# A one-element memset on GpSimd that waits for TensorE's reads ahead of the cast of keys, in an attention kernel

## Chip, cores and metric

The kernel runs on one core of a Trainium2 chip. The metric is device time in microseconds of one execution, the median of several. Times inside an execution come from a hardware profile of one run and count from the start of its span. Engines are named TensorE (PE in the profile, with its weight loads as PEld), VectorE (DVE), ScalarE (ACT), GpSimd (POOL) and SyncE (SP).

## What is computed

Plain softmax attention over 64 heads of 512 positions by 64 numbers, in float32 at both ends:

```python
batch, heads, seq, dim = 8, 8, 512, 64
scores = np.einsum('bhqd,bhkd->bhqk', q, k) * scale      # scale = 1 / sqrt(dim)
scores = scores - scores.max(axis=-1, keepdims=True)
attn = np.exp(scores)
attn = attn / attn.sum(axis=-1, keepdims=True)
return np.einsum('bhqk,bhkd->bhqd', attn, v).astype(np.float32)
```

## The kernel before

Two heads form a pair; there are 32 pairs, counted by `g`. For each pair the kernel does this:

1. SyncE loads q, k and v of the pair, 256 KB each (`load`, line 462), into float32 tiles, seven of each kind.
2. GpSimd casts them to 16 bits (`cast`): q and k into one tile `qkp` for the pair (line 478; the pool of these tiles has five buffers), v into one of twelve tiles `vp` (line 468). Pair 0 is handled apart, by `first_pair`.
3. TensorE transposes q and k out of `qkp` into PSUM in eight steps (`transposes`, line 502), and VectorE copies the result to SBUF as `tqk` (`copy`, line 515).
4. TensorE multiplies blocks of keys with the queries into score tiles `st` of 128x1024 in PSUM (`scores`, line 542), of which there are three buffers.
5. ScalarE takes the exponential of most score tiles (line 546). For 16 of them VectorE builds the exponential instead: `raise_` reads the scores out of PSUM (line 566), then five passes over 16-bit tiles in SBUF finish it (`pass_`, lines 583, 592, 600, 602, 606).
6. TensorE multiplies the exponentials with `vp` (`values`, line 638). VectorE takes a reciprocal of the sums (line 612) and normalises into the tile `ring` (line 617), and a store carries each head out.

The order of all this is made ahead of time, by the class `Plan`. It walks through time in steps of 5 ns with a cost for each kind of work and writes a list of steps; these are then issued in that order, and every engine works through its own queue in order. The plan casts pair `g` only when the transposes of pair `g - QK16`, with `QK16 = 5`, are over, since the five `qkp` buffers are used in turn.

A cast is also placed against VectorE's work. The plan emits it ahead of a VectorE step that works out of PSUM, and `cast_behind` ties it to the VectorE instruction recorded last (`latest`), with a dependency whose reason reads "SBUF ports". So a cast of GpSimd normally waits for up to four things: its load, that VectorE instruction, TensorE's transposes which read the old contents of its `qkp` buffer, and GpSimd's own earlier writes to that buffer. The last two fall to the cast of keys, which is the first to write the buffer; the cast of queries writes the other half behind it. GpSimd's queue executes a wait as a separate semaphore instruction when an instruction has more than it carries itself.

Of the kernel before, what the change touches and what calls it, by code (L numbers as in the profile page):

```python
# [9 lines left out]
FP32 = mybir.dt.float32  # L10
# [371 lines left out]
def kernel(  # L382
# [7 lines left out]
    nc = tc.nc  # L390
    B, H, S, D = q.shape
    P = 128
# [18 lines left out]
    cpool = ctx.enter_context(tc.tile_pool(name="const", bufs=1))  # L411
# [15 lines left out]
    ident = cpool.tile([P, P], FP16, name="ident")  # L427
# [3 lines left out]
    qkp = {}  # L431
    tqk = {}
    tps = {}
# [30 lines left out]
    def cast(g, name):  # L464
        if g >= NP:
            return
        if name == "v":
            return nc.gpsimd.tensor_copy(  # L468
                out=vps[g % NV][:, :, :, 0:D], in_=raw[g]["v"][:, :, :, :]
            )  # L470
        if g not in qkp:
            qkp[g] = qpool.tile([P, 2, NI, P], FP16, tag="qkp", name=f"qkp_{g}")
        dst = qkp[g][:, "qk".index(name)].rearrange("p i (h d) -> p h i d", h=2)
        src = raw[g][name]
        if (g, name) == (1, "q"):
            nc.vector.tensor_copy(out=dst[:, :, 0:2], in_=src[:, :, 0:2])
            return nc.gpsimd.tensor_copy(out=dst[:, :, 2:4], in_=src[:, :, 2:4])
        return nc.gpsimd.tensor_copy(out=dst, in_=src[:, :, :, :])  # L478

    latest = []
    SYNC = mybir.DependencyInfo(mybir.DependencyClass.Sync, mybir.DependencyReason.DATA)

    def dve(ins):
# [1 line left out]
        return ins  # L487

    def cast_behind(g, name, behind):
        ins = cast(g, name)  # L490
        if behind and latest:
            tc.add_manual_dep(ins.ins, latest[0].ins.name, SYNC, reason="SBUF ports")

    def transposes(g, n, bank):
        if n == 0:
            tqk[g] = tpool.tile([P, 2, S], FP16, tag="tqk", name=f"tqk_{g}")
        if n == 0 or g == 1:

            tps[g] = ps_x.tile([P, 2, NI, P], FP16, tag=f"x{bank ^ n}", name=f"tp_{g}_{n}")
        n = 1 - n  # L500
        for i in range(NI):
            nc.tensor.transpose(tps[g][:, n, i, :], qkp[g][:, n, i, :], ident)  # L502
        if g == 1 and n == 1:
            copy(g, n)

    def copy(g, n=0):
        if g == 1:
            dve(
                nc.vector.tensor_copy(
                    out=tqk[g][:, n], in_=tps[g][:, n].rearrange("p i c -> p (i c)")  # L510
                )
            )
            return
        dve(
            nc.vector.tensor_copy(  # L515
                out=tqk[g][:, :, :], in_=tps.pop(g).rearrange("p n i c -> p n (i c)")
            )
        )
# [258 lines left out]
    with tc.manual_schedule():  # L777
        plan = Plan(groups, NP, 3)
        steps = plan.run()
        first_loads()  # L780
        for g, name in plan.first_loads:
            load(g, name)
        make_identity(nc, ident)
        for n in range(NV):
            nc.vector.memset(vps[n][:, :, :, D : D + 1], 1.0)
        first_pair()
        do = {
            "transposes": transposes,
            "scores": scores,
            "values": values,  # L790
            "load": load,
            "store": store,
            "cast": cast_behind,
            "raise": raise_,
            "copy": lambda g, b: copy(g),
            "pass": pass_,
            "last": last_values,
            "finish": finish,
            "rec": lambda u, n, b: reciprocal(u, n),
            "mul": lambda u, n, b: normalise(u, n),  # L800
        }
        for what, *args in steps:
            do[what](*args)
# [30 lines left out]
```

## Time and profile before

| | |
|---|---|
| median of 3 runs | 115.96 us (115.36 to 116.09) |
| the profiled execution | 115.99 us, of which the span of instructions is 114.2 us |
| TensorE busy | 104.4 us, 91% of the span |
| VectorE busy | 103.3 us, 90% |
| ScalarE busy | 106.5 us, 93% |
| GpSimd busy | 56.8 us, 50% |
| granted TensorE clock, mean | 0.998 |
| casts of keys, line 478 | 31, 616 ns each |
| casts of queries, line 478 | 30, 616 ns each |
| casts of values, line 468 | 32, 619 ns each |

A row of the timeline gives the start and the duration in us, the engine, the line in the kernel, the operation, the tile written and the tile read, and in brackets the idle time of the engine before it with the instruction that ended it. A row of groups gives, behind the count, the busy time in us and the mean of one in ns, and then the idle time before the group's instructions. A row of one line's instructions gives the minimum, median and maximum in ns. A row of windows gives the stretch, its length, and the busy time of PE, PEld, DVE, ACT and POOL, each with its count, then clock, DMA share and rate. Recorded spans of one engine can overlap, since an instruction starts before the one ahead has ended.

### The profile page before, as it was taken

Reading aid. Unit: us, or ns where it says so; the run is one execution under the profiler, and the core shown is the slowest. Engines: PE = TensorE matmul, PEld = TensorE weight load, DVE = VectorE, ACT = ScalarE, POOL = GpSimd, SP = SyncE. Lnnn points to the kernel's source line nnn. Section 1 sums busy time; section 2 is a strip of 40 time slices with the busy share of each in tenths; the row PEclk is TensorE's granted clock in tenths of the full one; section 3 lists DMA queues with packets and bytes.
Section 4 is the critical chain, followed back from the end, with each engine's and each line's share of the span. In section 5 each row is a group of like instructions: output and inputs, shape, how many; then the busy total and the mean of one; then the engine's idle time right before and its main releaser. Section 6 shows DMA issues by size and latency. Waiting matters only on the chain.

```text
span 114.2 us, 4337 instructions
## 1 busy us (share of the span) xinstructions
PE 104.4 (91%) x1687; PEld 67.9 (59%) x1687; DVE 103.3 (90%) x226; ACT 106.5 (93%) x118; POOL 56.8 (50%) x101
## 2 busy tenths in 40 slices
PE   7966999999999889999999999999999999999950
PEld 2623566566856457666658557567675676577640
DVE  1557899999999999999999999999999999999660
ACT  4698999999999999999999999999999999999940
POOL 2156844785445744784473675655828374400000
PEclk9999999999999999999999999999999999999999
DMA  2899999999999999789899999999995993755243
GB/s 94 277 359 379 384 386 375 384 380 378 384 354 350 354 375 354 259 268 302 216 374 361 305 277 329 326 350 349 366 322 165 301 291 121 260 182 187 98 149 130
DMA packets 35381, 33.84 MB, mean 296 GB/s; under 512 B 2592, under 2 KB 35360, under 8 KB 35360
## 3 DMA queue, kind: packets, MB, share of 16 engines
q1 hardware_dynamic: 34928, 33.17, 87.3%
q10 hardware_dynamic: 432, 0.39, 1.0%
q8 instruction: 13, 0.21, 0.8%
q14 instruction: 8, 0.07, 0.2%
HBM read 25.17 MB, written 8.39 MB: 294 GB/s over the span
## 4 chain that ended last, share of the span: by engine, by line
DVE 50%; PE 20%; DMA 11%; ACT 9%; issue 4%; POOL 1%; SPq 1%; ACTq 0%
PE o L638 10%; DVE pd L566 10%; DVE tqk L515 10%; DVE ring L617 9%; ACT pt L546 9%; PE st L542 8%; DVE m L600 5%; DMA q<-in_q_dram 5%; DVE pd L606 4%; DMA out_dram<-ring 4%; DVE pe L592 3%; DMA v<-in_v_dram 3%; DVE rc L612 2%; DVE m L602 2%; DVE m L583 2%
## 5 line engine op out<-in xcount | busy, mean ns | idle before, releaser
L546 ACT ACTIVATE pt<-st 128x1024 f16<-128x1024 f32 (+1 forms) x110 | 101.3, 1054 | 0.7 <-PE st L542 0.3
L638 PEld LDWEIGHTS <-pt 128*128 128x128 f16 x880 | 38.7, 98 | 13.0 <-issue 10.6
L638 PE MATMUL o<-vp,pt 128*128 128x65 f16 x880 | 45.5, 194 | 0.7 <-DVE ring L617 0.2
L542 PE MATMUL st<-tqk 64*128 64x512 f16 (+1 forms) x250 | 42.5, 381 | 2.2 <-ACT pt L546 0.7
L478 POOL CAST qkp<-k 128x512 f16<-128x512 f32 x31 | 19.1, 616 | 16.5 <-DVE pe L592 4.2
L468 POOL CAST vp<-v 128x512 f16<-128x512 f32 x32 | 19.4, 619 | 14.3 <-DVE m L602 4.3
L478 POOL CAST qkp<-q 128x512 f16<-128x512 f32 x30 | 18.5, 616 | 9.0 <-DVE pe L592 2.4
L638 PE MATMUL o<-vp,pe 128*128 128x65 f16 x128 | 22.2, 195 | 0.2
L617 DVE TENSOR_TENSOR ring<-o,rc 128x448 f32<-128x448 f32 (+2 forms) x37 | 22.1, 599 | 0.1
L638 PE MATMUL o<-vp,pd 128*128 128x65 f16 x128 | 22.0, 193 | 0.1
L502 PEld LDWEIGHTS <-qkp 128*128 128x128 f16 x248 | 14.2, 97 | 10.9 <-issue 5.2
L502 PE MATMUL tp<-ident,qkp 128*128 128x128 f16 x248 | 19.6, 220 | 1.3 <-DVE tqk L515 0.6
L566 DVE TENSOR_SCALAR pd<-st 128x1024 uint16<-128x1024 f32 x16 | 19.4, 1213 | 1.0 <-PE st L542 1.0
L515 DVE COPY tqk<-tp 128x1024 f16<-128x1024 f16 x30 | 20.2, 676 | 0.0
L542 PEld LDWEIGHTS <-tqk 64*128 64x128 f16 x250 | 10.6, 93 | 11.1 <-issue 3.0
L638 PEld LDWEIGHTS <-pe 128*128 128x128 f16 x128 | 12.5, 98 | 2.9 <-issue 2.0
L638 PEld LDWEIGHTS <-pd 128*128 128x128 f16 x128 | 12.6, 98 | 0.4 <-DVE pd L606 0.2
L600 DVE TENSOR_TENSOR m<-m 128x1024 f16<-128x1024 f16 x16 | 12.6, 787 | 0.0
L606 DVE TENSOR_TENSOR pd<-pd,m 128x1024 f16<-128x1024 f16 x16 | 11.8, 739 | 0.0
L612 DVE RECIPROCAL rc<-o 128x7 f32<-128x7 f32 (+2 forms) x37 | 7.1, 192 | 1.3 <-PE o L638 1.3
L592 DVE TENSOR_SCALAR pe<-pd 128x1024 uint16<-128x1024 uint16 x16 | 7.1, 446 | 0.0
L583 DVE TENSOR_SCALAR m<-pd 128x1024 uint16<-128x1024 uint16 x16 | 6.9, 434 | 0.0
(49 smaller groups left out, 31.0 us busy)
## 6 DMA issues: line engine op xcount, KB each, us to landing
v<-in_v_dram SPq DMA_DIRECT2D x32, 256.0 KB, 5.5
k<-in_k_dram SPq DMA_DIRECT2D x31, 256.0 KB, 5.4
q<-in_q_dram SPq DMA_DIRECT2D x31, 256.0 KB, 5.3
out_dram<-ring SPq DMA_DIRECT2D x62, 128.0 KB, 2.9
k<-in_k_dram ACTq DMA_DIRECT2D x2, 128.0 KB, 2.9
q<-in_q_dram SPq DMA_DIRECT2D x2, 128.0 KB, 2.7
out_dram<-ring ACTq DMA_DIRECT2D x1, 128.0 KB, 1.7
out_dram<-obl SPq DMA_DIRECT2D x1, 128.0 KB, 1.7
```

The source lines that it names most:

```text
L468: return nc.gpsimd.tensor_copy(out=vps[g % NV][:, :, :, 0:D], in_=raw[g]["v"][:, :, :, :])
L478: return nc.gpsimd.tensor_copy(out=dst, in_=src[:, :, :, :])
L502: nc.tensor.transpose(tps[g][:, n, i, :], qkp[g][:, n, i, :], ident)
L515: nc.vector.tensor_copy(out=tqk[g][:, :, :], in_=tps.pop(g).rearrange("p n i c -> p n (i c)"))
L542: nc.tensor.matmul(st[:, x, cols], kc, qc[:, cols], start=True, stop=True)
L546: nc.scalar.activation(out=pt[:, :, cols], in_=st[:, :, cols], func=EXP, scale=scale, bias=SHIFT)
L566: nc.vector.tensor_scalar(out=r["pd"][:, :, :], in0=r["st"][:, :, :], scalar1=BITS, scalar2=BIAS, op0=AluOp.mult, op1=AluOp.add,)
L592: ins = nc.vector.tensor_scalar(out=r["pe"][:, :, :], in0=u[:, :, :], scalar1=0x7C00, scalar2=None, op0=AluOp.bitwise_and,)
L600: ins = nc.vector.tensor_tensor(out=m16, in0=m16, in1=m16, op=AluOp.mult)
L606: ins = nc.vector.tensor_tensor(out=u16, in0=u16, in1=m16, op=AluOp.mult)
L617: nc.vector.tensor_tensor(out=ring[:, u % NU : u % NU + n, :], in0=o[:, x : x + n, 0:D], in1=rcs.pop(u)[:, 0:n].broadcast_to([P, n, D]), o ...
L638: nc.tensor.matmul(os[u // 7][:, u % 7, :], part[:, y * P : (y + 1) * P], vps[g % NV][:, h, c, :], start=(n == 0), stop=(n == len(parts) - 1),
```

## The change

Ahead of the cast of keys of pair `g`, GpSimd now sets one element of a new tile `mark` to zero. A dependency makes this memset wait for the last transpose of pair `g - 5`, the pair that used the same `qkp` buffer before. `transposes` keeps that instruction in `reads`. As pair 0 has no such transposes, the first memset stands ahead of the cast of keys of pair 6, and there are 26 in all. Once the memset has waited, the cast behind it in GpSimd's queue needs no wait for TensorE.

```diff
     latest = []
+    reads = {}
+    mark = cpool.tile([P, 1], FP32, name="mark")
...
     def cast_behind(g, name, behind):
+
+
+        if name == "k" and g - Plan.QK16 in reads:
+            small = nc.gpsimd.memset(mark[0:1, :], 0.0)
+            tc.add_manual_dep(small.ins, reads[g - Plan.QK16].ins.name, SYNC, reason="tile")
         ins = cast(g, name)
         if behind and latest:
             tc.add_manual_dep(ins.ins, latest[0].ins.name, SYNC, reason="SBUF ports")
...
         for i in range(NI):
-            nc.tensor.transpose(tps[g][:, n, i, :], qkp[g][:, n, i, :], ident)
+            reads[g] = nc.tensor.transpose(tps[g][:, n, i, :], qkp[g][:, n, i, :], ident)
```

## Prediction

> **What bounds the kernel now.** I read the page's busy shares first, then the stretches by window, the chain that ended last, and only then the rows of single instructions around the casts.
>
> ```profile
> PE 104.4 (91%) x1687; PEld 67.9 (59%) x1687; DVE 103.3 (90%) x226; ACT 106.5 (93%) x118; POOL 56.8 (50%) x101
> DVE 50%; PE 20%; DMA 11%; ACT 9%; issue 4%; POOL 1%; SPq 1%; ACTq 0%
> ...
> 12.00:107.00 95.00, 92.00 (x1551) 60.88 (x1549) 94.70 (x191) 94.69 (x104) 51.78 (x88) 1.00 0.93 309
> 107.00:114.20 7.20, 3.10 (x75) 2.56 (x73) 2.69 (x8) 2.71 (x4) 0.00 (x0) 0.97 0.45 149
> ```
>
> The third number of a window row's busy times is VectorE, the fourth ScalarE. From 12 to 107 us VectorE is busy 94.70 of 95.00 us and ScalarE 94.69. VectorE has no gap to give, and its queue is in order; half of the chain is its own work. So whatever makes one VectorE instruction shorter moves all behind it, as far as ScalarE follows. The last 7.2 us are a tail that the change does not touch.
>
> ScalarE is as full, but not by work alone:
>
> ```profile
> 7.79 1.03 ACT L546 ACTIVATE pt<-st 128x1024 f16<-128x1024 f32 x1
> 9.17 8.36 ACT L546 ACTIVATE pt<-st 128x1024 f16<-128x1024 f32 x9 [0.34 <-PE st L542]
> ...
> 16.42 1.10 ACT L546 ACTIVATE pt<-st 128x1024 f16<-128x1024 f32 x1
> ...
> 17.33 1.11 ACT L546 ACTIVATE pt<-st 128x1024 f16<-128x1024 f32 x1
> ...
> 108.66 0.60 ACT L546 ACTIVATE pt<-st 128x512 f16<-128x512 f32 x1
> ...
> L546 ACT ACTIVATE pt<-st 128x1024 f16<-128x1024 f32 (+1 forms) x110 | 101.3, 1054 | 0.7 <-PE st L542 0.3
> ```
>
> When its scores are ready, one exponential follows another by 0.91 us (17.33 - 16.42), their recorded spans overlapping. The exponential at 16.42 is the tenth of 110 (one, then nine), the one at 108.66 the 109th. Between them lie 99 steps, or 90.1 us at 0.91, but 92.24 us pass. So about 2.1 us is the most that ScalarE can give back, in waits which the overlapping spans hide. That caps any gain here.
>
> **Where VectorE loses time.** Its passes over 16-bit tiles have a shortest and a usual length (minimum, median, maximum in ns):
>
> ```profile
> L583 DVE TENSOR_SCALAR m<-pd x16: 369/414/589, 11.1 to 103.3; 128x1024 uint16<-128x1024 uint16 x16
> L592 DVE TENSOR_SCALAR pe<-pd x16: 369/412/615, 13.7 to 104.2; 128x1024 uint16<-128x1024 uint16 x16
> L600 DVE TENSOR_TENSOR m<-m x16: 633/777/1033, 14.4 to 104.5; 128x1024 f16<-128x1024 f16 x16
> L602 DVE TENSOR_SCALAR m<-m x16: 369/422/501, 16.0 to 105.3; 128x1024 f16<-128x1024 f16 x16
> L606 DVE TENSOR_TENSOR pd<-pd,m x16: 640/706/921, 16.6 to 106.1; 128x1024 f16<-128x1024 f16 x16
> ```
>
> The long ones stand beside a cast of GpSimd. One place shows it:
>
> ```profile
> 16.64 0.68 DVE L606 TENSOR_TENSOR pd<-pd,m 128x1024 f16<-128x1024 f16 x1
> 17.24 0.68 DVE L515 COPY tqk<-tp 128x1024 f16<-128x1024 f16 x1
> 17.84 0.59 DVE L592 TENSOR_SCALAR pe<-pd 128x1024 uint16<-128x1024 uint16 x1
> 18.35 0.19 DVE L612 RECIPROCAL rc<-o 128x7 f32<-128x7 f32 x1
> 18.47 0.63 DVE L600 TENSOR_TENSOR m<-m 128x1024 f16<-128x1024 f16 x1
> ...
> 17.54 0.62 POOL L478 CAST qkp<-k 128x512 f16<-128x512 f32 x1 [1.43 <-DVE pd L606]
> 19.16 0.62 POOL L478 CAST qkp<-q 128x512 f16<-128x512 f32 x1 [1.01 <-DVE m L600]
> ...
> L478 POOLq EVENT_SEMAPHORE  x3: 17/17/43, 17.4 to 17.5; - x3
> ```
>
> A cast is released by the end of a chosen VectorE instruction, so that it runs beside a copy out of PSUM. The cast of keys was released at 17.32 (16.64 + 0.68) and began at 17.54, 0.22 us later; it then ran to 18.16, past the copy's end at 17.92, and the pass at 17.84 took 0.59 instead of 0.37. The cast of queries was released at 19.10 and began at 19.16, 0.06 us later. The difference is 0.16 us, and the last row names it: GpSimd's queue handles separate semaphore waits ahead of the cast of keys, one after the other, and starts that only when VectorE has finished.
>
> **The change part by part.** The built order of the changed kernel differs on GpSimd alone: 26 memsets, one ahead of each cast of keys from pair 6 on. Each takes over the wait for TensorE, and with it, from the second on, the wait for GpSimd's own earlier writes. The casts keep a DMA wait and mostly a VectorE wait, the form that casts of queries have; the first keeps one wait more. The order on TensorE, VectorE, ScalarE and the load queue is the same.
>
> *Gain.* In the trace, 15 of the 26 casts of keys start 0.22 us after the VectorE instruction that releases them; the first is at 17.54, the last at 92.58:
>
> ```profile
> 92.28 0.68 DVE L515 COPY tqk<-tp 128x1024 f16<-128x1024 f16 x1
> 92.88 1.21 DVE L566 TENSOR_SCALAR pd<-st 128x1024 uint16<-128x1024 f32 x1
> ...
> 91.89 0.62 POOL L478 CAST qkp<-q 128x512 f16<-128x512 f32 x1 [1.01 <-DVE pe L592]
> 92.58 0.62 POOL L478 CAST qkp<-k 128x512 f16<-128x512 f32 x1
> ...
> L478 POOL CAST qkp<-k 128x512 f16<-128x512 f32 x26 | 16.0, 616 | 13.8 <-DVE pe L592 4.2 <-PE st L542 2.7 <-DVE pd L606 2.2
> ```
>
> Ten of the fifteen have GpSimd idle before them for longer than 0.2 us, as at 17.54, and a delayed pass behind them, at once or after casts that follow without a gap: 10 x 0.16 = 1.6 us less delay on VectorE. The first keeps a separate wait for VectorE and saves about 0.1. Four come 0.02 to 0.07 us after the cast before (92.58 is one: 91.89 + 0.62 = 92.51), so GpSimd itself is free only then; they save 0.04 to 0.09 each, 0.3 together. Three more with fewer waits start 0.12 after their release and save 0.1 together. Sum 2.1 us.
>
> *Price.* The trace has no memset of one element. The nearest rows:
>
> ```profile
> 0.24 0.10 POOL L818 MEMSET const-float32-0.0<- 128x1 f32 x1 [0.24 <-issue]
> 0.27 0.10 POOL L818 MEMSET const-float32-1.0<- 128x1 f32 x1
> ...
> 0.73 0.20 POOL masks.py:197 MEMSET ident<- 128x128 f16 x1 [0.29 <-POOLq L818]
> ...
> 23.09 0.62 POOL L478 CAST qkp<-k 128x512 f16<-128x512 f32 x1
> 23.66 0.62 POOL L478 CAST qkp<-q 128x512 f16<-128x512 f32 x1
> ```
>
> One element per partition takes 0.10 us and delays the next memset by 0.03; a whole 128x128 tile takes 0.20. I take 0.04 of queue time, near the low end, since one element is nearest to those rows, with 0.03 and 0.20 as ends. In the idle places the memset runs right behind the cast before, over a microsecond ahead of the release, and costs GpSimd nothing; without that idle time it would cost its queue time. Behind it in GpSimd's queue stands the cast of keys, then those of queries and values, and the loads that reuse their tiles; none of them waits longer for TensorE than before, since the cast itself held that wait. Eight memsets stand between casts that follow each other closely (23.09 is such a cast of keys), where 0.04 shifts a pass by 0.02 to 0.04: 0.25. At about five places a 16-bit pass of VectorE is waiting for the cast ahead to end when the memset follows; between nothing and 0.10 each, I take 0.05: 0.25. Below nothing the price cannot be, as the memset replaces no work.
>
> The Trainium skill bears on these five. "SBUF — State Buffer", section "Who interferes with whom", says that a GpSimd instruction and a VectorE pass in a two-port mode exclude each other, for the whole instruction, whichever starts first. By it a memset that got in ahead would hold up the pass for all of its 0.10: 0.5 instead of 0.25, and the net on VectorE would be 1.35 us and the time 115.0. The same section lets VectorE instructions with two inputs in SBUF collide only with GpSimd instructions that read SBUF, which a memset does not.
>
> Net on VectorE: 2.1 - 0.25 - 0.25 = 1.6 us. How much of that reaches the end? At least VectorE's share of the chain, 50%; at most all, as 1.6 is under the 2.1 that ScalarE can give. I take three quarters, 1.2 us, for ScalarE's waits are spread over the whole span and follow VectorE's lateness. The profiled execution took 115.99 us (span 114.2 and 1.8 around it), so 115.99 - 1.2 = 114.8. The median of the runs shown is 115.96 (115.36 to 116.09), so the same sum holds for it: 1.0% faster. About 1% is also what a measurement of this kernel can tell from no change.
>
> **The rivals.**
> 1. *VectorE gains, the end hardly moves.* For it: TensorE is busy 92.00 of 95.00 us from 12 to 107, and half of the chain is not VectorE's. Against it: VectorE never waits there. A quarter of 1.6 arrives: 115.6.
> 2. *All of it arrives.* The memset is hidden everywhere and earlier casts also release transposes earlier; ScalarE gives back 1.9 of its 2.1: 114.1.
> 3. *Slower: the memset blocks.* It costs as much as the memset at 0.73, 0.20 us, and each of the 26 gets between VectorE's passes or pushes a cast out of its place: 26 x 0.20 = 5.2, less 2.1, is 3.1 lost, of which three quarters, 2.3, arrive: 118.3. It decides from 2.1 / 26 = 0.08 us a memset on. For it: GpSimd's casts do hold up VectorE (0.59 for 0.37). Against it: the rows of one element, and that most memsets fall in idle time.
> 4. *The change does not do what it says*, the cast still starts 0.22 late because something other than its separate waits delays it: 116.0.
>
> **How the numbers follow.** Forecast 0.45, rival 1 0.20, rival 2 0.18, rival 3 0.14, rival 4 0.03. The forecast's own range (a half to all of 1.6) is 114.4 to 115.2; 1% faster is 114.8, and I put 0.30 of its 0.45 on that side, as casts of queries and transposes behind an earlier cast of keys also gain. With rival 2 that is 0.48 for faster. Slower by over 1% is rival 3 but for its cheap end, 0.12. The rest is 0.40. The range goes from 113.9, just below rival 2 and the cap of 2.1, to 116.7, where each memset costs VectorE about 0.12 (26 x 0.12 - 2.1 = 1.0, three quarters of it 0.75); it leaves most of rival 3 out.
>
> **What would show it.** Casts of keys behind idle time start 0.06 us after their release; memsets take about 0.1 us and lie right behind the cast before; the five kinds of pass lose less (the medians above fall, the pass near 17.8 us to about 0.49, as the cast beside it saves 0.1); VectorE stays without gaps and ScalarE's last exponential comes 1.2 us earlier. Wrong would be: 0.22 still there (rival 4), the passes shorter but ScalarE's last exponential where it was (rival 1), or passes longer beside memsets (rival 3).

## The result, and the profile after

The changed kernel takes 115.03 us in the median of 20 executions, the kernel before 115.86 us in the median of 20. Over the executions that compare, the ratio is 0.993, with a 95% interval of 0.9912 to 0.9948: 0.7% faster, clear of the noise, and under the 1% that was forecast. The time lies inside the range of the prediction, but its larger chance, 0.48, stood on more than 1%; the measured gain falls to the 0.40 in the middle. In a later series the ratio was 0.9922 (0.9898 to 0.9946). One execution of the change, at 117.95 us and a granted clock of 0.967, is left out of the ratios.

Two executions of the changed kernel are profiled. The first (114.50 us, span 112.7) began its first casts some 0.4 us earlier than the profile before did, for its first loads came sooner. The second (114.66 us, span 112.9) started like the profile before, so the comparison is made with that one. The five kinds of pass and the memset there, as rows of one line's instructions (minimum, median, maximum in ns):

```profile
L590 DVE TENSOR_SCALAR m<-pd x16: 369/415/514, 11.1 to 102.0; 128x1024 uint16<-128x1024 uint16 x16
L599 DVE TENSOR_SCALAR pe<-pd x16: 368/375/586, 13.7 to 102.8; 128x1024 uint16<-128x1024 uint16 x16
L607 DVE TENSOR_TENSOR m<-m x16: 633/698/1033, 14.5 to 103.2; 128x1024 f16<-128x1024 f16 x16
L609 DVE TENSOR_SCALAR m<-m x16: 367/424/500, 16.0 to 103.9; 128x1024 f16<-128x1024 f16 x16
L613 DVE TENSOR_TENSOR pd<-pd,m x16: 635/692/771, 16.7 to 104.8; 128x1024 f16<-128x1024 f16 x16
...
L495 POOL MEMSET mark<- x26: 88/88/373, 16.1 to 91.1; 1x1 f32 x26
```

Lines 590, 599, 607, 609 and 613 are what 583, 592, 600, 602 and 606 were before. The shortest passes are as short as they were. Three of the five medians have come down (412 to 375, 777 to 698 and 706 to 692 ns), two have not moved, and the longest `m<-m` of 1033 ns stands ahead of the first memset. The place near 17.8 us, from the timeline:

```profile
16.70 0.68 DVE L613 TENSOR_TENSOR pd<-pd,m 128x1024 f16<-128x1024 f16 x1
17.30 0.68 DVE L522 COPY tqk<-tp 128x1024 f16<-128x1024 f16 x1
17.90 0.49 DVE L599 TENSOR_SCALAR pe<-pd 128x1024 uint16<-128x1024 uint16 x1
...
16.11 0.37 POOL L495 MEMSET mark<- 1x1 f32 x1
17.50 0.61 POOL L478 CAST qkp<-k 128x512 f16<-128x512 f32 x1 [1.02 <-issue]
```

The cast of keys is released at 17.38 (16.70 + 0.68) and starts at 17.50: 0.12 us later instead of 0.22, as this first cast keeps one separate wait. The pass behind it takes 0.49 instead of 0.59. The memset lies far ahead, in GpSimd's idle time. The next place shows the full step, first before, then after:

```profile
30.03 0.37 DVE L592 TENSOR_SCALAR pe<-pd 128x1024 uint16<-128x1024 uint16 x1
30.86 0.92 DVE L600 TENSOR_TENSOR m<-m 128x1024 f16<-128x1024 f16 x1
...
30.62 0.62 POOL L478 CAST qkp<-k 128x512 f16<-128x512 f32 x1 [1.50 <-DVE pe L592]
```

```profile
29.89 0.37 DVE L599 TENSOR_SCALAR pe<-pd 128x1024 uint16<-128x1024 uint16 x1
30.71 0.77 DVE L607 TENSOR_TENSOR m<-m 128x1024 f16<-128x1024 f16 x1
...
28.91 0.09 POOL L495 MEMSET mark<- 1x1 f32 x1
30.32 0.61 POOL L478 CAST qkp<-k 128x512 f16<-128x512 f32 x1 [1.32 <-DMA q<-in_q_dram]
```

Before, 0.22 us from the release (30.40) to the start; after, 0.06 (30.26 to 30.32). The pass behind it falls from 0.92 to 0.77 us. Before, two separate semaphore instructions ran behind the release, at 30.44 and 30.50. After, the cast still has one, for its load, but it ran at 28.40, ahead of the release, and costs nothing. (The bracket of the last row is the profile's guess; both loads of this pair had landed by 26 us.)

### The profile page after: what moved, and what is told of

It reads as the page before. It is cut to its first block, busy times and chain, and to the rows that moved or that the text cites. A ratio compares the mean times of both kernels' runs of the same rounds, so it can differ in the third digit from the quotient of the medians.

```text
span 112.7 us, 4366 instructions
## 1 busy us (share of the span) xinstructions
PE 103.6 (92%) x1687; PEld 67.7 (60%) x1687; DVE 102.2 (91%) x226; ACT 105.7 (94%) x118; POOL 58.7 (52%) x127
## 4 chain that ended last, share of the span: by engine, by line
PE 47%; DVE 38%; ACT 7%; issue 3%; DMA 1%; DVEq 0%; ACTq 0%
PE o L645 20%; PE st L549 17%; DVE pd L573 8%; DVE tqk L522 7%; ACT pt L553 7%; PE tp L509 7%; DVE ring L624 6%; DVE m L607 4%; PE st_0a L692 3%; DVE pd L613 3%; DVE pe L599 2%; DVE m L590 2%; DVE m L609 2%; DVE rc L619 2%; DMA out_dram<-ring 1%
## 5 line engine op out<-in xcount | busy, mean ns | idle before, releaser
L607 DVE TENSOR_TENSOR m<-m 128x1024 f16<-128x1024 f16 x16 | 11.6, 728 | 0.0
L613 DVE TENSOR_TENSOR pd<-pd,m 128x1024 f16<-128x1024 f16 x16 | 11.3, 707 | 0.0
```

The costliest lines, as they stand in the source:

```text
L607: ins = nc.vector.tensor_tensor(out=m16, in0=m16, in1=m16, op=AluOp.mult)
L613: ins = nc.vector.tensor_tensor(out=u16, in0=u16, in1=m16, op=AluOp.mult)
```

## The experiments

Each was timed over five rounds beside the kernel before on the same chip. The ratios are to that kernel, with 95% intervals.

**The wait on the cast ahead, without a memset.**

```diff
     latest = []
+    reads = {}
+    ahead = []
...
     def cast_behind(g, name, behind):
+        if name == "k" and g - Plan.QK16 in reads:
+            tc.add_manual_dep(ahead[0].ins, reads[g - Plan.QK16].ins.name, SYNC, reason="tile")
         ins = cast(g, name)
+        ahead[:] = [ins]
...
```

> No memset; the wait for TensorE's reads is put on the cast that stands just ahead of the cast of keys in GpSimd's queue. The cast of keys then has three waits instead of four, one separate semaphore instruction instead of two. Theory (the late start of the casts of keys is what VectorE pays): they start 0.12 us after their release instead of 0.22, up to 15 x 0.10 = 1.5 us less delay on VectorE, some of it lost where the cast ahead now starts 0.12 after its own release; about half arrives as with the changed kernel: 0.3 to 0.6 us faster than before, some 115.4. Rival (the memset itself, by breaking up GpSimd's queue, is what helps): no change, 115.9.

Measured: 115.33 us, ratio 0.9966 (0.9937 to 0.9995), so 0.4 us faster, as the theory had it. At the same place as above, from the timeline of this kernel:

```profile
30.66 0.37 DVE L597 TENSOR_SCALAR pe<-pd 128x1024 uint16<-128x1024 uint16 x1
31.49 0.82 DVE L605 TENSOR_TENSOR m<-m 128x1024 f16<-128x1024 f16 x1
...
31.16 0.62 POOL L478 CAST qkp<-k 128x512 f16<-128x512 f32 x1 [1.40 <-DVE pe L597]
```

The start is 0.13 us after the release (31.03), and the pass takes 0.82. With 0.22, 0.13 and 0.06 us of lateness the pass takes 0.92, 0.82 and 0.77: the lateness of the cast is passed on nearly in full. No memset is needed for a gain.

**The memset alone.** The dependency line of the change is left out.

> The 26 memsets stand where the change puts them but wait for nothing of TensorE; the casts of keys keep all their waits. Theory: the casts still start 0.22 us late, the passes stay as long as before, and the memsets cost 0 to 0.5 us on VectorE, so 115.9 to 116.3. Rival (the memset itself helps): about 115.0 like the changed kernel.

Measured: 115.10 us, ratio 0.9943 (0.9918 to 0.9968). The rival's number came out, but not for the rival's reason, and the expectation was wrong on what the edit does. All memsets write the same element, so each still waits for GpSimd's own writes up to the memset before it. That covers the wait for the older write of the buffer, and the casts of keys drop it. They start 0.12 us after their release, and the pass at the place above takes 0.82, as in the run before. The next run takes that apart.

**The memset apart from every wait.** As the run before, but each memset has an element of its own:

```diff
+    mark = cpool.tile([P, 32], FP32, name="mark")
...
+        if name == "k" and g - Plan.QK16 in reads:
+            nc.gpsimd.memset(mark[0:1, g : g + 1], 0.0)
```

> The 26 memsets wait for nothing and each sets an element of its own, so they carry no wait of GpSimd's own either, and the casts of keys keep all four waits and both separate semaphore instructions. This parts the memset from the waits, which the memset-only run did not: there the wait for GpSimd's own writes still moved to the memset, and the casts started 0.12 us after release. Theory: casts start 0.22 us late again, and what is left is the price of the memsets, 0 to 0.4 us slower than before: 115.8 to 116.2. Rival (a memset in the queue helps by itself): 115.1, as with the memset alone.

Measured: 116.13 us, ratio 1.0037 (1.0017 to 1.0057). The casts start 0.22 us late again and nothing is gained; the rival falls. At the same place the release is at 30.23 and the pass takes 0.92 again:

```profile
29.86 0.37 DVE L598 TENSOR_SCALAR pe<-pd 128x1024 uint16<-128x1024 uint16 x1
30.69 0.92 DVE L606 TENSOR_TENSOR m<-m 128x1024 f16<-128x1024 f16 x1
...
30.45 0.62 POOL L478 CAST qkp<-k 128x512 f16<-128x512 f32 x1 [1.48 <-DVE pe L598]
```

The kernel is even 0.4 us slower. Two more runs split that between the two kinds of place, with the condition in the edit above changed to lists of pairs.

> The memset alone cost 0.4 us in the run with all 26 apart from the waits. Here only the eight of them that stand between casts which follow each other closely; all casts of keys keep their four waits. Theory: the price lies here, 8 x 0.03 to 0.04 us of shift on VectorE and three quarters of it at the end: 0.2 us slower than before. Rival (the price lies where the memset meets a waiting pass, behind idle time): no change.

Measured, with the eight between close casts: 116.06 us, ratio 1.0028 (1.0007 to 1.0049).

> The other 18 memsets alone, those ahead of casts of keys that start after idle time or a release of VectorE; all casts of keys keep their four waits. Theory: 0 to 0.1 us slower than before. Rival (they get between VectorE's passes, 0.05 us and more at some five places, or push casts out of place): 0.3 to 0.4 us slower.

Measured, with the other 18: 116.05 us, ratio 1.0021 (0.9996 to 1.0046). The timings do not tell the two apart. In the profile of the first one the eight memsets, from 23.6 us on, delay VectorE by nothing to speak of: ahead of them it is already 0.48 us behind the profile before (a normalising instruction at 24.00 instead of 23.52), and at its last pass 0.49 (106.62 instead of 106.13). The profile of the second one shows a different culprit:

```profile
20.09 1.21 DVE L572 TENSOR_SCALAR pd<-st 128x1024 uint16<-128x1024 f32 x1
21.22 0.67 DVE L521 COPY tqk<-tp 128x1024 f16<-128x1024 f16 x1
21.82 0.19 DVE L618 RECIPROCAL rc<-o 128x7 f32<-128x7 f32 x1
21.93 1.06 DVE L612 TENSOR_TENSOR pd<-pd,m 128x1024 f16<-128x1024 f16 x1
...
21.34 0.09 POOL L495 MEMSET mark<- 1x1 f32 x1
21.84 0.61 POOL L478 CAST qkp<-k 128x512 f16<-128x512 f32 x1 [0.41 <-DMA k<-in_k_dram]
```

This is the cast of keys of pair 7. The VectorE instruction that releases it ended at 21.30, the memset was over at 21.43, and the cast waited on for its load, which landed at 21.69 (19.94 in the profile before). It then met a pass, which took 1.06 us instead of 0.65. Behind this place no VectorE instruction of this profile differs in length by more than 0.02 us from the profile before. So in these two traces the memsets cost nothing to speak of, and in the second a late load did. What makes the medians of the three versions with memsets apart from the waits 0.2 to 0.4 us slower stays open.

**Only where a cast is late.** The change, but with memsets only ahead of 18 of the casts of keys:

```diff
-        if name == "k" and g - Plan.QK16 in reads:
+        if name == "k" and g in (6, 7, 9, 10, 12, 13, 14, 16, 17, 18, 20, 21, 23, 24, 26, 28, 30, 31):
```

> As the change, but only ahead of the 18 casts of keys that start after idle time or a release of VectorE; the eight that follow closely on another cast (pairs 8, 11, 15, 19, 22, 25, 27, 29) get no memset and keep their waits. Theory: their waits are handled while the cast ahead still runs and cost nothing, so the memsets there were pure price: 0 to 0.3 us faster than the changed kernel, 114.7 to 115.0. Rival (each cast of keys gains by losing its waits): the eight are late again, 8 x 0.16 on VectorE, half arriving: 115.6.

Measured: 114.73 us, ratio 0.992 (0.9885 to 0.9954). It was run again beside the change itself:

> The changed kernel once more, on the chip of the run below: 115.0.

> The version with memsets only ahead of 18 casts of keys, once more, to compare with the changed kernel on one chip. Theory: 0.1 to 0.3 us faster than the changed kernel. Rival: no difference.

Measured: the change 114.76 us, ratio 0.9922 (0.9898 to 0.9946); the 18 memsets 114.85 us, ratio 0.9922 (0.9894 to 0.995). No difference: the eight memsets between close casts gain nothing, and cost too little to see.

**A longer memset.** The change with `mark` as a 128x128 tile of 16 bits, all of it set.

> As the change, but each memset writes a 128x128 tile of 16 bits instead of one element; such a memset took 0.20 us in the trace of before. Theory (most memsets lie in idle time of GpSimd, only the some ten between close casts cost): 10 x 0.11 us more than the changed kernel on VectorE, of which half to all arrives: 115.5 to 116.1, still not slower than before. Rival 3 of the prediction (every memset over 0.08 us is paid by VectorE): 26 x 0.20 - 2.1 = 3.1 us lost, three quarters of it arriving: 118.2.

Measured: 116.21 us, ratio 1.0042 (1.0016 to 1.0068), just above the theory's range and far from rival 3. That it would still not be slower than before was wrong. The memset takes 0.20 us, and here it does get ahead of waiting passes:

```profile
15.90 0.58 DVE L609 TENSOR_SCALAR m<-m 128x1024 f16<-128x1024 f16 x1
...
16.00 0.20 POOL L495 MEMSET mark<- 128x128 f16 x1
...
L495 POOL MEMSET mark<- x26: 203/205/207, 16.0 to 92.7; 128x128 f16 x26
```

The same pass takes 0.44 us beside the memset of one element. Between close casts the long memset also shifts the next cast by 0.15 us. So its length does matter; at 0.09 us the change gains, at 0.20 it loses.

**How much of VectorE's time reaches the end.**

```diff
+        elif s == 3 and m in Plan.ON_DVE[2::3]:
+            return
         elif s == 3:
             ins = nc.vector.tensor_scalar(
```

> The kernel before, with the pass of line 602 left out for five of the 16 tiles that VectorE raises (its result is left out for them), which takes 5 x 0.34 = 1.7 us out of VectorE's queue at other places than the casts. It measures how much of VectorE's time reaches the end. Prediction's three quarters: 1.3 us faster, 114.5. Rival (ScalarE, TensorE and the waits between them hold the end): half or less, 115.0 to 115.4.

Measured: 114.58 us, ratio 0.9892 (0.9869 to 0.9916). On 115.87 us that is 1.25 us of the 1.7 taken out, 74%, with the interval from 57% to 89%. But more than 1.7 was taken out: the means of the other four kinds of pass fell too, from 434, 446, 787 and 739 ns to 432, 438, 779 and 720, which is 37 ns together, or 0.6 us over 16 tiles. Of 2.3 us, 1.25 is a little over half. So this run does not bear out the three quarters; it puts the share at about a half to three quarters.

**Where the late load comes from.** The rate of the transfers from 8 to 20 us (last number of a window row) in the profile before, in the change run again, and in two more versions below:

```profile
8.00:20.00 12.00, 10.38 (x142) 6.12 (x143) 10.69 (x21) 11.66 (x13) 7.23 (x12) 1.00 1.09 381
```

```profile
8.00:20.00 12.00, 10.29 (x143) 6.17 (x142) 10.84 (x22) 11.77 (x14) 7.55 (x13) 1.00 1.09 349
```

Ahead of the first memset the change already loads more slowly. What differs there is memory: `mark` takes 4 bytes of each partition, is given 32, and moves all tiles allocated after it. In the built kernel before, the load tiles begin at multiples of 256 bytes (the first tile of keys at 64256 in its partition, 251 x 256); behind `mark` they do not (64288 in the change, 64384 where `mark` is 128 bytes wide). Two versions test it. One makes `mark` 256 bytes wide in the change, still setting one element; the other only sets `mark` aside in the kernel before.

```diff
-    mark = cpool.tile([P, 1], FP32, name="mark")
+    mark = cpool.tile([P, 64], FP32, name="mark")
```

> The change with the tile of the memset made 256 bytes wide in each partition instead of 4; the memset still sets one element. In the profiles so far the loads ran at 376 to 381 GB/s from 8 to 20 us where the load tiles begin at a multiple of 256 bytes (the kernel before, the wait put ahead, the pass left out, the full tile), and at 349 to 354 where the new tile has moved them off it (all eight with a narrow tile). Theory (the small tile's place in memory, not the memset, is the rest of the price): loads at 375 to 385 GB/s, the cast of keys of pair 7 never late, and 0.2 to 0.4 us faster than the changed kernel: 114.5 to 114.7. Rival (the two rates belong to the hour or the chip): 349 GB/s and 115.0.

> The kernel before with the tile of the change set aside in memory and never used: no memset, no changed wait, only the tiles behind it moved by 32 bytes. Theory: loads at 349 GB/s from 8 to 20 us, the cast of keys of pair 7 late in some executions, 0.2 to 0.4 us slower than before: 116.0 to 116.3, which is what the runs with memsets apart from the waits showed. Rival (the memsets themselves cost that): no change, 380 GB/s.

```profile
8.00:20.00 12.00, 10.39 (x144) 6.12 (x143) 10.74 (x21) 11.00 (x13) 7.72 (x14) 1.00 1.09 382
```

```profile
8.00:20.00 12.00, 10.30 (x144) 6.13 (x140) 10.73 (x21) 11.79 (x14) 7.23 (x13) 1.00 1.09 350
```

The rate follows the place of the tiles: 382 GB/s for the widened tile, 350 for the kernel before with the tiles moved. What it is worth in time is not shown: the first took 114.57 us, ratio 0.9901 (0.987 to 0.9932), the lowest median of all versions but within the intervals of the change; the second 115.89 us, ratio 1.0012 (0.998 to 1.0043), no difference. The expected 0.2 to 0.4 us are not borne out by it.

## Why the prediction held, step by step

**The late start and its cause: right.** Casts behind idle time start 0.06 us after their release instead of 0.22, the first one 0.12. The two runs that leave casts with one separate wait gave the step between, and the memset apart from the waits gave 0.22 again.

**The gain on VectorE: the mechanism right, the net too small.** The groups of the passes, before and in the change run again, with the mean of one in ns:

```profile
L592 DVE TENSOR_SCALAR pe<-pd 128x1024 uint16<-128x1024 uint16 x16 | 7.1, 446 | 0.0
L583 DVE TENSOR_SCALAR m<-pd 128x1024 uint16<-128x1024 uint16 x16 | 6.9, 434 | 0.0
L602 DVE TENSOR_SCALAR m<-m 128x1024 f16<-128x1024 f16 x16 | 6.7, 417 | 0.0
L600 DVE TENSOR_TENSOR m<-m 128x1024 f16<-128x1024 f16 x16 | 12.6, 787 | 0.0
L606 DVE TENSOR_TENSOR pd<-pd,m 128x1024 f16<-128x1024 f16 x16 | 11.8, 739 | 0.0
```

```profile
L599 DVE TENSOR_SCALAR pe<-pd 128x1024 uint16<-128x1024 uint16 x16 | 6.7, 420 | 0.0
L590 DVE TENSOR_SCALAR m<-pd 128x1024 uint16<-128x1024 uint16 x16 | 6.7, 420 | 0.0
L609 DVE TENSOR_SCALAR m<-m 128x1024 f16<-128x1024 f16 x16 | 6.7, 416 | 0.0
L607 DVE TENSOR_TENSOR m<-m 128x1024 f16<-128x1024 f16 x16 | 11.7, 728 | 0.0
L613 DVE TENSOR_TENSOR pd<-pd,m 128x1024 f16<-128x1024 f16 x16 | 11.3, 707 | 0.0
```

The five means sum to 2823 ns before and 2691 after; times 16, VectorE's passes are 2.1 us shorter, with all costs of the memsets already in. The forecast had 2.1 before costs and 1.6 after them.

**The price of the memsets: too high on VectorE.** Queue time between close casts is 0.04 us, as taken (22.84 and 22.88 in the first profile of the change). But the 0.25 for these eight places did not arrive at VectorE: with the memsets there alone, its lateness grew by 0.01 us. The 0.25 for the places with a waiting pass did not fall due either: there are four such places, the memset waited, 0.37 us instead of 0.09, and the pass took as long as before (0.44, at one place 0.38 for 0.40). This agrees with the rule cited from the Trainium skill, "SBUF — State Buffer", section "Who interferes with whom", that one of the two shuts out the other for the whole instruction; but the pass went first at these places with one element, and the memset of a full tile did.

**The share that arrives: the step that was off.** Of 2.1 us, VectorE's last pass kept 1.36 (106.13 before, 104.77 after), and ScalarE's 109th exponential came 1.34 us earlier:

```profile
106.13 0.68 DVE L606 TENSOR_TENSOR pd<-pd,m 128x1024 f16<-128x1024 f16 x1
```

```profile
104.77 0.68 DVE L613 TENSOR_TENSOR pd<-pd,m 128x1024 f16<-128x1024 f16 x1
...
107.32 0.60 ACT L553 ACTIVATE pt<-st 128x512 f16<-128x512 f32 x1
```

That is 65% instead of 75%. From the first of the 16-bit passes to the last it is 95.00 us before (11.13 to 106.13) and 93.70 in the second profile of the change; the first profile with 18 memsets (11.06 to 104.76) and that with the widened tile (11.69 to 105.39) give 93.70 as well, so the 1.3 us do not hang on one pair of profiles. (Two others, in which the load of keys of pair 7 comes late, the first profile of the change among them, give 94.0 and 94.1.) Most of the rest, 0.6 us, went into waits that VectorE did not have before, at seven places behind a normalising instruction, ahead of four reciprocals and three copies; both kinds read what TensorE has just written. One place, first before, then after:

```profile
48.90 0.61 DVE L617 TENSOR_TENSOR ring<-o,rc 128x448 f32<-128x448 f32 x1
49.43 0.19 DVE L612 RECIPROCAL rc<-o 128x7 f32<-128x7 f32 x1
```

```profile
48.33 0.62 DVE L624 TENSOR_TENSOR ring<-o,rc 128x448 f32<-128x448 f32 x1
48.96 0.21 DVE L619 RECIPROCAL rc<-o 128x7 f32<-128x7 f32 x1
...
48.73 0.19 PE L645 MATMUL o<-vp,pt 128*128 128x65 f16 x1
```

The reciprocal started 0.53 us behind the normalising instruction, and now 0.63, when the matmul at 48.73 is over. This is a part of rival 1, at some places: VectorE has come to where TensorE is the later one. The sign that VectorE stays without gaps did not come true. The profiled pair differs by 1.33 us (115.99 to 114.66), the medians by 0.8 to 1.1. In single executions luck with loads adds to or takes from that: in the first profile of the change, the load of keys of pair 7 landed at 21.11, half a microsecond after the release of its cast at 20.60 (the bracket names a copy that ended at 21.20). The cast then stood beside a pass and took 1.10 us, and a pass behind it took 0.81.

```profile
21.23 1.10 POOL L478 CAST qkp<-k 128x512 f16<-128x512 f32 x1 [0.50 <-DVE tqk L522]
...
23.57 0.81 DVE L590 TENSOR_SCALAR m<-pd 128x1024 uint16<-128x1024 uint16 x1
```

So the sum came near for two errors that offset each other: a net on VectorE that was too small, 1.6 for 2.1, and a share that was too large, three quarters for two thirds or less. That they nearly cancel is luck. How far slower loads hold down the medians stays open, as the shift alone showed no difference in time.

**Rivals.** Rival 2 (all of it arrives) did not happen. Rival 3's point, 0.08 us a memset, was set too low: the memset is recorded at 0.09 and the change gains, since most of them lie in idle time and the others hardly reach VectorE; the 0.20 of the full tile was enough for a loss, of 0.4 us and not 2.3. Rival 4 falls with the first rows above.

## What to carry to other kernels

Where an instruction is meant to start just when another engine ends, count its waits: the ones that do not fit into it run one after the other, and those that come behind the wait that ends last delay the start, here by 0.16 us each time; one that is over earlier costs nothing. Any cheap instruction ahead of it in the same queue can take the old waits, as long as it is short and falls in idle time. When an experiment moves a wait, look at which waits the built instructions still carry before saying what the run tests: here the memset alone moved one too. And a small helper tile can be given a size that leaves the tiles behind it where they were; here that kept the rate of the loads, though no gain in time was shown.

## What the runs showed that was not expected

The loads ran faster into tiles that begin at a multiple of 256 bytes in the partition: the rate from 8 to 20 us was 376 to 382 GB/s with it (5 profiles) and 349 to 354 where they begin 32 or 128 bytes off (9 profiles). No effect on the kernel's time was shown. The Trainium skill, "DMA: Bandwidth & Descriptors", section "How a descriptor splits into AXI transactions", says that a descriptor which does not start at a 256-byte boundary begins its first transaction at the boundary below and pays for the unused bytes. The page says this of bytes that are fetched; here it is the written end that moved, and no run shows whether the rule holds for that end too. If it did, for pieces of 1 KB, as these loads have, it would be five transactions instead of four and, as an estimate from that page, some 3% more beats; the runs show a loss of 8% (381 to 349). So the direction is the same, the size does not follow from it, and the cause stays open. The prediction did not look at where the new tile lies.

A memset of one element and one of a full tile behave differently when a 16-bit pass of VectorE already waits behind the cast ahead: the small one lets the pass go first and ends 0.37 us after its start, the large one ends after its usual 0.20 and the pass takes 0.58 instead of 0.44. Why was not tried.
